# Level products of a gated scan in quarters of the TensorE array, and one place for turning attention's queries

## The chip, the core and the metric

One NeuronCore of a Trainium2 chip runs the whole block as one program. The metric is the device time of one execution in microseconds. A run is one execution; the median of the runs is the time quoted. The profile is one further execution, whose trace is read here.

TensorE (PE) multiplies: a weight load puts one operand into the array, then a matmul streams the other one past it. In the profile the two are PEld and PE. VectorE is DVE, ScalarE is ACT, GpSimd is POOL, and SP issues most of the loads.

## The reference, cut to what matters

A sequence of 256 tokens and a context of 256 tokens pass one block of width 2048: a modulated norm, one wide projection `w_in`, a window attention branch, a gated scan branch in both directions (16 heads of 128), and two output projections that are merged. The change touches the scan and the attention.

```python
def hgrn2_scan(q, k, v, logf, s0):            # forward; the backward one runs on flipped tokens
    def step(S, inp):                         # chunks of 64 tokens
        qc, kc, vc, gc = inp
        G = jnp.cumsum(gc, axis=2)
        o_inter = einsum('bhtk,bhkv->bhtv', qc * jnp.exp(G), S)
        decay = jnp.exp(jnp.where(causal, G_t - G_s, -jnp.inf))
        A = einsum('bhtk,bhsk,bhtsk->bhts', qc, kc, decay)
        o = o_inter + einsum('bhts,bhsv->bhtv', A, vc)
        ...
o = o_f + flip(o_b)                           # hgrn2_bidir
...
q = apply_axial_rope(aq, cos, sin) * HEAD_DIM ** -0.5      # window_attention: 16 heads,
p = softmax(q k^T over 256 tokens in a window + 256 of context, with a sink)   # 4 key heads
att_branch = (p v) * silu(ag)
```

What counts for the change is the matrix A, queries by keys, in both directions at once. Each of its entries carries the decay between its two tokens.

## The kernel before, in words

Every projection takes a weight chunk in `wchunk`: SP loads it, ACT rounds it to a high part `wh`, DVE subtracts to get the low part `wl`, and PE runs three products for each output (`mm3`, lines 82 to 84). All of PE's instructions stand in the order in which the code emits them. The other engines' order comes from the scheduler, which goes by priority.

**The scan.** `pair` handles two heads at a time, so there are 8 pairs. It is a generator: at each `yield` the caller `weave` emits so many projection matmuls of the next pair (the filler), and then the pair goes on. The 256 tokens of two heads make four blocks of 128 by 128 on A's diagonal (index `a`), and four blocks off the diagonal. `AT` holds all eight, keys on the partitions. The diagonal blocks are built in levels: level `b` holds the products of keys and queries in sibling blocks of `b` tokens inside one block of `2b`; level 0 is a token with itself. `grow` multiplies the decay of one more level into queries and keys on DVE; `copies` sets aside on ACT what a level needs.

A level is made by `level` on PE and stored by `keep`. In PSUM the tiles are called `al`. Before the change a level is 8 matmuls: for each `a`, two halves of the array (`tile_position` 0 and 64), 64 keys by 64 queries of fp32. The trace shows an fp32 matmul as two records, so a level is 16 records of PE and 16 of PEld. A pair has two stretches of PE with four levels each: 0, 1, 2, 4 and then 8, 16, 32, 64. `keep` writes the level straight into its place in `AT`: ACT copies levels 0 and 64, one instruction for each half, and DVE writes the others through a mask `mk` (line 570), also one for each half. After the second stretch come four matmuls for the blocks off the diagonal (lines 661 and 662), an ACT copy of them (line 665), 1.5 steps of filler, and then the outputs `ob` (line 677), which read `AT`.

**The attention.** `attend` walks over 32 steps (4 groups of 4 heads, 2 halves of the tokens), and at each yield one piece of `fill` is emitted. A step computes scores `sc`; two steps later its probabilities are turned (`tkp`), and every fourth step multiplies them by the values into `oba`. `group_in(j)` is the filler for group `j`: 8 chunks of the query projection, then 8 of the gate projection. The queries get their rotation on DVE (`rope`), and `turn_q(t)` turns them on PE into the PSUM tile `tkq`, for both halves `t`; ACT and DVE then split that tile into `qTa` (lines 925 and 926). `tkq` and `oba` take turns in the one PSUM buffer with the tag `o`: whichever comes next on PE waits until the one ahead has been read. The table `TURNS` says after which of the 8 gate chunks each half is turned, for each group.

Of the kernel before, what the change touches and what calls it, by code (L numbers as in the profile page):

```python
# [19 lines left out]
EPS = 1e-6  # L20
NEG = -3.0e38
PRIO = 100000
# [8 lines left out]
K_SIN = K_COS + 2 * HD  # L31
K_TRI = K_SIN + 2 * HD
K_END = K_TRI + 2 * P
LEVELS = (1, 2, 4, 8, 16, 32, 64)


@with_exitstack
def block_kernel(ctx: ExitStack, tc: tile.TileContext, x, c, cx, c_ctx, w_ada, b_ada, norm_gain, w_in,
                 b_merge, lb_f, lb_b, hg_gain, w_oh, sink, w_oa, w_out, fin_gain, cst, msk, out):
    nc = tc.nc  # L40
    pe, act, dve, pool = nc.tensor, nc.scalar, nc.vector, nc.gpsimd
# [116 lines left out]

    cs = few.tile([P, K_END], F32, name="cs")
    ident = cs[:, K_ID: K_ID + P]  # L160
    mk = pad.tile([P, 8, P], U8, name="mk")
    mhalf = pad.tile([P, 8], F32, name="mhalf")
    pool.memset(mhalf, -0.5)

# [54 lines left out]
    with pl("st", reuse_waits="tile") as st:  # L219
        cT = st.tile([P, KT, 32], F32, name="cT")  # L220
        mod = st.tile([P, 2, KT, 2], F32, name="mod")
        rows = st.tile([48, P], F32, name="rows")
# [221 lines left out]
        with tc.manual_schedule(engines={mybir.EngineType.PE, mybir.EngineType.SP}):  # L444
# [4 lines left out]
            hi = proj_tok_g(w_in, C_HI, x_st, range(4))  # L449
            bv0 = result(hi)  # L450
            nc.sync.dma_start(cs[:, P:], cst[:, P:])
        mkf = wp.tile([P, 1024], F32, tag="raw", name="mkf", bufs=4)
        nc.sync.dma_start(mkf, msk)
        dve.tensor_copy(mk.rearrange("p a b -> p (a b)"), mkf)

# [18 lines left out]
    def pair(g, p, grp, F, banks_q):  # L474
# [49 lines left out]
        kslot = {1: Kmt[:, 0], 2: Kmt[:, 1], 4: fc[0], 8: Kmt[:, 0], 16: qk[:, 0], 32: F[0][:, :, :T], 64: accT[:, 1]}  # L524
        qslot = {1: fc[1], 2: accT[:, 1], 8: Kmt[:, 1], 16: qk[:, 1], 32: fc[0]}
# [9 lines left out]
                    else:  # L535
                        act.activation(dst.rearrange("p (n two b) -> p n two b", two=2, b=b), src, AF.Copy)  # L536

        def cut(slot, t0):

            return slot[:, t0 // T, t0 % T: t0 % T + 64] if len(slot.shape) == 3 else slot[:, t0: t0 + 64]  # L540

        def level(al, z, b):

            for a in range(4):
                for c in range(2):
                    s0 = a * P + 64 * c
                    t0 = s0 if b < 64 else a * P + 64 * (1 - c)
                    o = al[64 * c: 64 * c + 64, z * 256 + a * 64: z * 256 + a * 64 + 64]  # L550
                    if b == 0:
                        ky, mv = ksum[:, s0: s0 + 64], qT[:, s0: s0 + 64]
                    elif b in qslot:
                        ky, mv = cut(kslot[b], s0), cut(qslot[b], t0)
                    else:
                        ky = cut(kslot[b], s0)
                        o = o.rearrange("p (n two b) -> p n two b", two=2, b=b)
                        mv = mix(1, 1, t0, 64, b)
                    pe.matmul(o, ky, mv, start=True, stop=True, tile_position=(0, 64 * c))  # L559

        def keep(al, z, b):
            for c in range(2):
                hf = slice(64 * c, 64 * c + 64)
                tf = hf if b < 64 else slice(64 * (1 - c), 64 * (1 - c) + 64)
                src = al[hf, z * 256: z * 256 + 256].rearrange("p (a b) -> p a b", a=4)
                if b in (0, 64):
                    act.activation(AT[hf, 0:4, tf], src, AF.Copy)
                else:
                    m = mk[hf, LEVELS.index(b), tf].unsqueeze(1).to_broadcast([64, 4, 64])
                    dve.copy_predicated(AT[hf, 0:4, tf], m, src)  # L570

        tots = {}

# [31 lines left out]
            tots[2 * b] = Tn  # L605

        AT = X2[:, :1024].rearrange("p (a t) -> p a t", a=8)
        TT = X2[:, 1024:]

        def al_bank():  # L610
            return ps.tile([P, 512], F32, tag=alt(), name="al")
# [30 lines left out]
        grow(2)  # L642
        copies(4)
        yield 1.5
        a1, a2 = al_bank(), al_bank()
        for al, z, b in ((a1, 0, 0), (a1, 1, 1), (a2, 0, 2), (a2, 1, 4)):
            level(al, z, b)
        for b in (4, 8, 16, 32):
            grow(b)
            copies(2 * b)  # L650
        grow(64)
        for al, z, b in ((a1, 0, 0), (a1, 1, 1), (a2, 0, 2), (a2, 1, 4)):
            keep(al, z, b)
        yield 3.0
        a3, a4 = al_bank(), al_bank()
        for al, z, b in ((a3, 0, 8), (a3, 1, 16), (a4, 0, 32), (a4, 1, 64)):
            level(al, z, b)
        a5 = ps.tile([P, 512], F32, tag="o", name="al")
        for i in range(2):
            t0, t1 = slice(i * T, i * T + P), slice(i * T + P, (i + 1) * T)  # L660
            pe.matmul(a5[:, 2 * i * P: (2 * i + 1) * P], A[:, 0, t0], A[:, 2, t1], start=True, stop=True)
            pe.matmul(a5[:, (2 * i + 1) * P: (2 * i + 2) * P], A[:, 3, t1], A[:, 1, t0], start=True, stop=True)
        for al, z, b in ((a3, 0, 8), (a3, 1, 16), (a4, 0, 32), (a4, 1, 64)):
            keep(al, z, b)
        act.activation(AT[:, 4:8, :], a5.rearrange("p (a b) -> p a b", a=4), AF.Copy)
        grow(128)
        yield 1.5
# [202 lines left out]
    with tc.manual_schedule(engines={mybir.EngineType.PE}):  # L870
# [25 lines left out]
        for t in range(4):  # L896
            rows = slice(8 + 2 * t, 10 + 2 * t)
# [9 lines left out]
                split(dst[0], dst[1], tk.rearrange("p (j t) -> p j t", j=4))  # L907
                yield

        TURNS = ((1, 3), (1, 4), (0, 3), (2, 4))

        def group_in(j, st):

            bq = yield from proj_tok_g(w_in, C_Q + 512 * j, x_st, range(2))
            def turn_q(t):
                qr = base.tile([P, 4, HD], F32, tag="bb", name="qr", bufs=2)
                rope(qr, bq[t], t)
                yield  # L920
                tk = ps.tile([P, 512], F32, tag="o", name="tkq")
                for i in range(4):
                    pe.transpose(tk[:, i * P: (i + 1) * P], qr[:, i, :], ident)
                qh, ql = [X[:, t].rearrange("p h t -> p (h t)") for X in st["q"]]
                act.activation(qh, tk, AF.Copy, scale=HD ** -0.5)
                dve.scalar_tensor_tensor(ql, tk, HD ** -0.5, qh.bitcast(F32), op0=ALU.mult, op1=ALU.subtract)

            turning = [turn_q(t) for t in range(2)]
            next(turning[0])
            st["q"] = [at.tile([P, 2, 4, P], F32R, tag=tg, name="qTa") for tg in Q_TAGS[j % 2]]  # L930
            st["g"] = gt_tile(j, [P, 4, T], "ga")
            for hf in range(2):
                bg = proj_col_x_g(w_in, C_G + 512 * j + 256 * hf)
                for k0 in range(0, KT, 4):
                    next(bg)
                    yield
                    if (hf, k0) == (0, 0):
                        next(turning[1])
                    for t in range(2):
                        if 4 * hf + k0 // 4 == TURNS[j][t]:  # L940
                            next(turning[t], None)
                for i, b in enumerate(result(bg)):
                    gs = halves_sum(b, "bb", 2)
                    gi = st["g"][:, 2 * hf + i, :]
                    act.activation(gi, gs, AF.Sigmoid)
                    dve.tensor_tensor(gi, gi, gs, op=ALU.mult)
# [139 lines left out]
    for k0 in range(0, KT, 4):  # L1086
        raw, _ = wload(w_out, k0 * P, 4, (D - 256,), 256)
# [10 lines left out]
    for t in range(2):  # L1098
# [7 lines left out]
        for c0, c1, on_act in ((0, 512, True), (512, 1024, False), (1024, 1536, True), (1536, D, False)):  # L1106
# [12 lines left out]
def _constants():  # L1119
    import numpy as np  # L1120

    cst = np.zeros((P, K_END), np.float32)
    cst[:, K_ID: K_ID + P] = np.eye(P, dtype=np.float32)
    tok = np.arange(T)
    row, col = (tok // 64).astype(np.float32), (tok % 64).astype(np.float32)
    inv = (1.0 / (np.float32(10000.0) ** (np.arange(0, 64, 2, dtype=np.float32) / np.float32(64)))).astype(np.float32)
    ar, ac = row[:, None] * inv[None], col[:, None] * inv[None]
    ang = np.concatenate([ar, ar, ac, ac], axis=-1).astype(np.float32)
    sign = np.repeat(np.array([-1, 1, -1, 1], np.float32), 32)
    cos, sin = np.cos(ang), np.sin(ang) * sign  # L1130
    for t in range(2):
        cst[:, K_COS + t * HD: K_COS + (t + 1) * HD] = cos[t * P: (t + 1) * P]
        cst[:, K_SIN + t * HD: K_SIN + (t + 1) * HD] = sin[t * P: (t + 1) * P]
    i, j = np.arange(P)[:, None], np.arange(P)[None, :]
    cst[:, K_TRI: K_TRI + P] = np.where(i >= j, 0.0, NEG)
    cst[:, K_TRI + P: K_TRI + 2 * P] = np.where(j >= i, 0.0, NEG)
    msk = np.zeros((P, 8, P), np.float32)
    for n, b in enumerate(LEVELS):
        msk[:, n] = (i // (2 * b) == j // (2 * b)) & (i // b != j // b)
    return cst, msk.reshape(P, 8 * P)  # L1140


# [27 lines left out]
```

## Time and profile before

| | before |
|---|---|
| median of 3 runs | 1663.74 us |
| lowest, highest | 1663.3, 1664.22 us |
| the profiled execution: its own time | 1663.35 us |
| its span, first to last instruction | 1661.6 us |
| mean granted TensorE clock | 0.995 |
| PE busy | 1631.7 us, 98% |
| DVE busy, ACT busy | 968.2 us, 744.7 us |

The scan's pairs lie between 200 and 910 us of the span, the attention between 1090 and 1460 us. Busy PE is what the matmuls' modelled ends cover: it can be busy and still run faster or slower, so the starts of its matmuls are read below, not only its busy time.

### The profile page before, as it was taken

To read this page: it belongs to the slowest core of one execution; us is meant where nothing else is said; L and a number is where in the kernel's file an instruction comes from. 1 tells how busy PE (TensorE), PEld (TensorE's weight loads), DVE (VectorE), ACT (ScalarE), POOL (GpSimd) and SP (SyncE) were. 2 spreads that over 40 slices of the span, in tenths; PEclk is the share of its full clock that TensorE was granted. 3 is DMA by queue.
4 is the path that set the end of the run, shared out by engine and by line. 5 is a ranking of instruction groups with operands and counts; after the bars stand their busy time and mean duration, and the time that the engine had idled before them with its cause. 6 is when DMAs were issued, how large, how long until landed. Compare 5 with 4: busy or idle time off the path is not lost.

```text
span 1661.6 us, 22807 instructions
## 1 busy us (share of the span) xinstructions
PE 1631.7 (98%) x8889; PEld 1346.9 (81%) x8889; DVE 968.2 (58%) x1503; ACT 744.7 (45%) x1133; POOL 34.8 (2%) x88
## 2 busy tenths in 40 slices
PE   7999999999999999999999999999999999999998
PEld 4558888888888888888888888888878878888887
DVE  4444577546665466745677455325667667555665
ACT  4333444324442344423455443224676767444443
POOL 2000000000000000000000000000000000000000
PEclk9999999999999999999999999999999999999999
DMA  9993444346343553435445556334534445665554
GB/s 354 381 386 108 151 141 140 102 135 191 93 126 116 161 169 102 129 113 176 105 129 171 182 190 194 123 102 145 173 119 149 131 144 159 213 215 190 188 191 140
DMA packets 191436, 275.22 MB, mean 166 GB/s; under 512 B 9808, under 2 KB 112480, under 8 KB 190560
## 3 DMA queue, kind: packets, MB, share of 16 engines
q1 hardware_dynamic: 189344, 269.39, 50.9%
q0 software_dynamic: 1264, 3.25, 1.0%
q8 instruction: 70, 1.15, 0.3%
q10 hardware_dynamic: 720, 1.11, 0.2%
q14 instruction: 38, 0.31, 0.1%
HBM read 271.61 MB, written 2.11 MB: 165 GB/s over the span
## 4 chain that ended last, share of the span: by engine, by line
PE 94%; DMA 3%; ACT 1%; DVE 1%; issue 1%; POOLq 0%; POOL 0%; SPq 0%; ACTq 0%
PE pj L82 23%; PE pj L84 23%; PE pj L83 23%; PE pj L140 7%; PE pj L145 4%; DMA raw<-in_w_ada_dram 3%; PE al L559 2%; PE pa L304 1%; PE pj L394 1%; PE sb L636 1%; PE tkp L978 1%; PE pj L387 1%; PE pj L388 1%; DMA X<-in_x_dram 0%; PE ob L677 0%
## 5 line engine op out<-in xcount | busy, mean ns | idle before, releaser
L76 DVE TENSOR_TENSOR wl<-raw,wh 128x1024 fp32r<-128x1024 f32 x392 | 479.3, 1223 | 432.4 <-ACT wh L75 431.9
L75 ACT ACTIVATE wh<-raw 128x1024 fp32r<-128x1024 f32 x392 | 414.8, 1058 | 590.6 <-PE pj L84 419.5
L83 PE MATMUL pj<-wl,xHL 128*128 128x512 f32 (+1 forms) x1024 | 395.5, 386 | 0.4 <-DVE wl L76 0.4
L84 PE MATMUL pj<-wh,xHL 128*128 128x512 f32 (+1 forms) x1024 | 395.4, 386 | 0.0
L82 PE MATMUL pj<-wh,xHL 128*128 128x512 f32 (+1 forms) x1024 | 391.0, 390 | 0.0
L84 PEld LDWEIGHTS pj<-wh,xHL 128*128 128x128 f32 x1024 | 192.4, 188 | 39.1
L83 PEld LDWEIGHTS pj<-wl,xHL 128*128 128x128 f32 x1024 | 192.5, 188 | 38.2 <-DVE wl L76 0.7
L82 PEld LDWEIGHTS pj<-wh,xHL 128*128 128x128 f32 x1024 | 192.2, 188 | 38.0 <-DVE yt L1034 0.4
L140 PE MATMUL pj<-xHL,wh 128*128 128x512 f32 x512 | 183.3, 400 | 0.0
L82 PE MATMUL pj<-xHL,wh 128*128 128x512 f32 x416 | 164.3, 395 | 0.0
L84 PE MATMUL pj<-xHL,wl 128*128 128x512 f32 x416 | 162.1, 390 | 0.0
L83 PE MATMUL pj<-xHL,wh 128*128 128x512 f32 x416 | 162.0, 390 | 0.0
L145 PE MATMUL pj<-xHL,wl 128*128 128x256 f32 x512 | 140.7, 285 | 0.0
L140 PEld LDWEIGHTS pj<-xHL,wh 128*128 128x128 f32 x512 | 96.4, 191 | 20.4
L145 PEld LDWEIGHTS pj<-xHL,wl 128*128 128x128 f32 x512 | 98.1, 192 | 2.7
L83 PE MATMUL pj<-wl,bH 128*128 128x512 f32 x256 | 99.9, 390 | 0.0
L84 PE MATMUL pj<-wh,bL 128*128 128x512 f32 x256 | 99.7, 389 | 0.0
L84 PEld LDWEIGHTS pj<-xHL,wl 128*128 128x128 f32 x416 | 78.1, 188 | 16.4
L83 PEld LDWEIGHTS pj<-xHL,wh 128*128 128x128 f32 x416 | 78.2, 188 | 15.5
L82 PEld LDWEIGHTS pj<-xHL,wh 128*128 128x128 f32 x416 | 78.2, 188 | 15.6
L82 PE MATMUL pj<-wh,bH 128*128 128x512 f32 x256 | 89.9, 390 | 0.1
L602 DVE TENSOR_TENSOR A<-A,X 128x512 f32<-128x512 f32 x96 | 62.0, 688 | 15.9 <-ACT so L536 6.1
(272 smaller groups left out, 1737.9 us busy)
## 6 DMA issues: line engine op xcount, KB each, us to landing
raw<-in_w_in_dram SPq DMA_DIRECT2D x292, 512.0 KB, 3.6
raw<-in_w_ada_dram SPq DMA_DIRECT2D x128, 256.0 KB, 5.5
raw<-in_w_ada_dram SPq DMA_DIRECT2D x32, 512.0 KB, 3.8
raw<-in_w_o_hgrn_dram SPq DMA_DIRECT2D x32, 512.0 KB, 3.7
raw<-in_w_o_attn_dram SPq DMA_DIRECT2D x32, 512.0 KB, 3.9
raw<-in_w_out_dram SPq DMA_DIRECT2D x32, 512.0 KB, 4.4
raw<-in_w_in_dram SPq DMA_DIRECT2D x24, 256.0 KB, 5.4
X<-in_x_dram SPq DMA_DIRECT2D x2, 1024.0 KB, 6.4
```

What stands on the lines that cost most here:

```text
L75: act.activation(h[:, :n], raw[:, :n], AF.Copy)
L76: dve.tensor_tensor(lo[:, :n], raw[:, :n], h[:, :n].bitcast(F32), op=ALU.subtract)
L82: pe.matmul(o, s[0], m[0], start=first, stop=False)
L83: pe.matmul(o, s[0], m[1], start=False, stop=False)
L84: pe.matmul(o, s[1], m[0], start=False, stop=last)
L140: pe.matmul(banks[i].rearrange("p (a t) -> p a t", a=2), h[:, j, cs_], xHL[:, :, kt, :T], start=kt == 0, stop=kt == KT - 1)
L145: pe.matmul(banks[i][:, :T], lo[:, j, cs_], xH[:, kt, :T], start=False, stop=False)
L304: pe.matmul(pa[32 * g: 32 * g + 32, : 2 * w], cT[:, k0 + g, :], rv_[:, :, g % nk, :], start=k0 == 0, stop=k0 == KT - 4, tile_position=(0, ...
L387: pe.matmul(o, hw, xH[:, kt, :], start=kt == 0, stop=False)
L388: pe.matmul(o, lo[:, kt - k, cs_], xH[:, kt, :], start=False, stop=False)
L559: pe.matmul(o, ky, mv, start=True, stop=True, tile_position=(0, 64 * c))
L602: dve.tensor_tensor(av, av, f.unsqueeze(3).to_broadcast([P, 2, n2, b]), op=ALU.mult)
```

## The change

Two things are changed.

**The levels.** Levels 0 to 32 become products of 32 keys by 32 queries, 16 matmuls in place of 8, in four quarters of the array (`tile_position` 0, 32, 64, 96). Level 32 pairs each 32 keys with the 32 queries of the sibling quarter. Level 64 becomes 16 matmuls of 32 keys by 64 queries. The results of levels 0 to 32 no longer go to their place in `AT`: all of them go to a compact tile `near`, 128 partitions by 4 by 64, which lies where `AT[:, 4:6]` will be. One instruction stores a level: ACT for levels 0 and 32, DVE with the mask for 1, 2, 4, 8, 16. The mask shrinks from 8 by 128 to 5 by 32 columns. A new function `spread` then copies `near` into `AT` on ACT with 8 instructions, one for each quarter and each of its two parts, ahead of the copy of the off-diagonal blocks. Level 64 still goes straight into `AT`. The four levels of the first stretch share one PSUM bank, and levels 8, 16, 32 another.

**The queries.** `TURNS` is gone: in each group the halves are turned after the gate chunks 1 and 3. Before it was (1, 3), (1, 4), (0, 3), (2, 4) for the groups 0 to 3. The two instructions that split `tkq` now stand at a raised priority.

```diff
-LEVELS = (1, 2, 4, 8, 16, 32, 64)
+LEVELS = (1, 2, 4, 8, 16)
...
-    mk = pad.tile([P, 8, P], U8, name="mk")
+    mk = pad.tile([P, len(LEVELS), 32], U8, name="mk")
...
-        def level(al, z, b):
+        def level(al, c0, b):
+            n = 64 if b == 64 else 32
             for a in range(4):
-                for c in range(2):
-                    s0 = a * P + 64 * c
-                    t0 = s0 if b < 64 else a * P + 64 * (1 - c)
-                    o = al[64 * c: 64 * c + 64, z * 256 + a * 64: z * 256 + a * 64 + 64]
+                for g in range(4):
+                    s0 = a * P + 32 * g
+                    t0 = a * P + (32 * (g ^ 1) if b == 32 else 64 * (1 - g // 2) if b == 64 else 32 * g)
+                    o = al[32 * g: 32 * g + 32, c0 + a * n: c0 + a * n + n]
...
-                    pe.matmul(o, ky, mv, start=True, stop=True, tile_position=(0, 64 * c))
+                    pe.matmul(o, ky, mv, start=True, stop=True, tile_position=(0, 32 * g))
...
+        def keep(al, c0, b):
+            if b == 64:
+                ...                                   # two ACT copies into AT, as before
+            src = al[:, c0: c0 + P].rearrange("p (a b) -> p a b", a=4)
+            if b in (0, 32):
+                act.activation(near[:, :, b: b + 32], src, AF.Copy)
+            else:
+                m = mk[:, LEVELS.index(b), :].unsqueeze(1).to_broadcast([P, 4, 32])
+                dve.copy_predicated(near[:, :, 0:32], m, src)
+        def spread():
+            for g in range(4):
+                rows = slice(32 * g, 32 * g + 32)
+                for z in range(2):
+                    c0 = 32 * (g ^ z)
+                    act.activation(AT[rows, 0:4, c0: c0 + 32], near[rows, :, 32 * z: 32 * z + 32], AF.Copy)
...
+        near = X2[:, 512:768].rearrange("p (a b) -> p a b", a=4)
...
-        TURNS = ((1, 3), (1, 4), (0, 3), (2, 4))
...
-                act.activation(qh, tk, AF.Copy, scale=HD ** -0.5)
-                dve.scalar_tensor_tensor(ql, tk, HD ** -0.5, ...)
+                with tc.high_priority(2 * PRIO):
+                    act.activation(qh, tk, AF.Copy, scale=HD ** -0.5)
+                    dve.scalar_tensor_tensor(ql, tk, HD ** -0.5, ...)
...
-                    for t in range(2):
-                        if 4 * hf + k0 // 4 == TURNS[j][t]:
-                            next(turning[t], None)
+                    if hf == 0 and k0 in (4, 12):
+                        next(turning[k0 // 8], None)
```

How the instructions stand, in three places. First PE in pair 0, second stretch of levels, before (`pj` is the filler's projection, `al` the levels):

```order
L84 MATMUL pj<-xHL,wl 128x512
L559 MATMUL al<-Kmt 64x64 x8
L559 MATMUL al<-qk 64x64 x8
L559 MATMUL al<-ff 64x64 x8
L559 MATMUL al<-so,acc 64x64 x8
L661 MATMUL al<-A 128x128
```

The same place after the change:

```order
L85 MATMUL pj<-xHL,wl 128x512
L562 MATMUL al<-Kmt 32x32 x16
L562 MATMUL al<-qk 32x32 x16
L562 MATMUL al<-ff 32x32 x16
L562 MATMUL al<-so,acc 32x64 x16
L677 MATMUL al<-A 128x128
```

Nothing else of PE's order moves in the scan: twice as many matmuls stand in each level's place, and the filler around them is the same.

Second, ACT in pair 1 behind the second stretch, before (`wh` is a weight chunk's high part, `X` is the buffer that holds `AT`, `sg` belongs to the next pair):

```order
L75 ACTIVATE wh<-raw 128x1024 x2
L665 ACTIVATE X_2250<-al 128x512
L567 ACTIVATE X_2250<-al 64x4x64 x2
L209 ACTIVATE sg<-pj 128x512
L75 ACTIVATE wh<-raw 128x1024
```

and after:

```order
L76 ACTIVATE wh<-raw 128x1024 x2
L569 ACTIVATE X_2315<-al 64x4x64 x2
L574 ACTIVATE X_2315<-al 128x4x32
L584 ACTIVATE X_2315<-X_2315 32x4x32 x8
L682 ACTIVATE X_2315<-al 128x512
L211 ACTIVATE sg<-pj 128x512
L76 ACTIVATE wh<-raw 128x1024
```

Nine instructions have come in between the level copies and `sg`, and the copy of the off-diagonal blocks now stands last.

Third, PE in attention group 1, where its second half of queries is turned, before:

```order
L83 MATMUL oba<-pT,xHL 128x512
L84 MATMUL oba<-pT,xHL 128x512
L978 MATMUL tkp<-cs,pr 128x128 x4
L923 MATMUL tkq<-cs,qr 128x128 x4
L145 MATMUL pj<-xHL,wl 128x256
```

and after:

```order
L83 MATMUL sc<-xHL,qTa 128x512
L84 MATMUL sc<-xHL,qTa 128x512
L85 MATMUL sc<-xHL,qTa 128x512
L936 MATMUL tkq<-cs,qr 128x128 x4
L141 MATMUL pj<-xHL,wh 128x512
```

`tkq` stood right behind `oba` and one turn of probabilities; it now stands behind the scores, 13 projection matmuls ahead of that same `oba`. Group 3 moves in the same way. In group 2 the second half stood there already, and only the first half moves.

Last, ACT in group 2 behind its second `tkq`, before (`ga` is the output gate, `pr` the probabilities):

```order
L945 ACT_TABLE_LOAD
L945 ACTIVATE ga<-hsum 128x256
L968 ACTIVATE pr<-pr,mx 128x512
L925 ACTIVATE qTa<-tkq 128x512
L154 ACTIVATE hsum<-pj 128x256
```

and after:

```order
L958 ACT_TABLE_LOAD
L958 ACTIVATE ga<-hsum 128x256
L939 ACTIVATE qTa<-tkq 128x512
L155 ACTIVATE hsum<-pj 128x256
L977 ACT_TABLE_LOAD
```

`qTa` has moved ahead of the scaling of `pr`. Groups 1 and 3 now have this order too.

More of the change, by code (lines that the diff above doesn't have):

```diff
@@ L160, in block_kernel @@
     ident = cs[:, K_ID: K_ID + P]
-    mk = pad.tile([P, 8, P], U8, name="mk")
+    mk = pad.tile([P, len(LEVELS), 32], U8, name="mk")
+    pad.tile([P, 216], F32, name="space0")
     mhalf = pad.tile([P, 8], F32, name="mhalf")
@@ L451, in block_kernel @@
             nc.sync.dma_start(cs[:, P:], cst[:, P:])
-        mkf = wp.tile([P, 1024], F32, tag="raw", name="mkf", bufs=4)
+        mkf = wp.tile([P, 1024], F32, tag="raw", name="mkf", bufs=4)[:, : 32 * len(LEVELS)]
         nc.sync.dma_start(mkf, msk)
@@ L536, in copies, with cut @@
                         act.activation(dst.rearrange("p (n two b) -> p n two b", two=2, b=b), src, AF.Copy)
-        def cut(slot, t0):
-            return slot[:, t0 // T, t0 % T: t0 % T + 64] if len(slot.shape) == 3 else slot[:, t0: t0 + 64]
-        def level(al, z, b):
+        def cut(slot, t0, n):
+            return slot[:, t0 // T, t0 % T: t0 % T + n] if len(slot.shape) == 3 else slot[:, t0: t0 + n]
+        def level(al, c0, b):
+            n = 64 if b == 64 else 32
             for a in range(4):
-                for c in range(2):
-                    s0 = a * P + 64 * c
-                    t0 = s0 if b < 64 else a * P + 64 * (1 - c)
-                    o = al[64 * c: 64 * c + 64, z * 256 + a * 64: z * 256 + a * 64 + 64]
[L551 to L559, printed above, removed]
@@ L561, in keep @@
-        def keep(al, z, b):
-            for c in range(2):
[L563 to L570, printed above, removed]
+                for g in range(4):
+                    s0 = a * P + 32 * g
+                    t0 = a * P + (32 * (g ^ 1) if b == 32 else 64 * (1 - g // 2) if b == 64 else 32 * g)
+                    o = al[32 * g: 32 * g + 32, c0 + a * n: c0 + a * n + n]
+                    if b == 0:
+                        ky, mv = ksum[:, s0: s0 + 32], qT[:, t0: t0 + 32]
+                    elif b in qslot:
+                        ky, mv = cut(kslot[b], s0, 32), cut(qslot[b], t0, n)
+                    else:
+                        ky = cut(kslot[b], s0, 32)
+                        o = o.rearrange("p (n two b) -> p n two b", two=2, b=b)
+                        mv = mix(1, 1, t0, n, b)
+                    pe.matmul(o, ky, mv, start=True, stop=True, tile_position=(0, 32 * g))
@@ new lines, in keep @@
+        def keep(al, c0, b):
+            if b == 64:
+                for c in range(2):
+                    hf = slice(64 * c, 64 * c + 64)
+                    act.activation(AT[hf, 0:4, 64 * (1 - c): 64 * (2 - c)],
+                                   al[hf, c0: c0 + 256].rearrange("p (a b) -> p a b", a=4), AF.Copy)
+                return
+            src = al[:, c0: c0 + P].rearrange("p (a b) -> p a b", a=4)
+            if b in (0, 32):
+                act.activation(near[:, :, b: b + 32], src, AF.Copy)
+            else:
+                m = mk[:, LEVELS.index(b), :].unsqueeze(1).to_broadcast([P, 4, 32])
+                dve.copy_predicated(near[:, :, 0:32], m, src)
@@ L644, in pair @@
         yield 1.5
-        a1, a2 = al_bank(), al_bank()
-        for al, z, b in ((a1, 0, 0), (a1, 1, 1), (a2, 0, 2), (a2, 1, 4)):
-            level(al, z, b)
+        a1 = al_bank()
+        for z, b in enumerate((0, 1, 2, 4)):
+            level(a1, z * P, b)
         for b in (4, 8, 16, 32):
@@ L651, in pair @@
         grow(64)
-        for al, z, b in ((a1, 0, 0), (a1, 1, 1), (a2, 0, 2), (a2, 1, 4)):
-            keep(al, z, b)
+        for z, b in enumerate((0, 1, 2, 4)):
+            keep(a1, z * P, b)
         yield 3.0
         a3, a4 = al_bank(), al_bank()
-        for al, z, b in ((a3, 0, 8), (a3, 1, 16), (a4, 0, 32), (a4, 1, 64)):
-            level(al, z, b)
+        for al, c0, b in ((a3, 0, 8), (a3, P, 16), (a3, 2 * P, 32), (a4, 0, 64)):
+            level(al, c0, b)
         a5 = ps.tile([P, 512], F32, tag="o", name="al")
@@ L662, in pair @@
             pe.matmul(a5[:, (2 * i + 1) * P: (2 * i + 2) * P], A[:, 3, t1], A[:, 1, t0], start=True, stop=True)
-        for al, z, b in ((a3, 0, 8), (a3, 1, 16), (a4, 0, 32), (a4, 1, 64)):
-            keep(al, z, b)
+        for al, c0, b in ((a3, 0, 8), (a3, P, 16), (a3, 2 * P, 32), (a4, 0, 64)):
+            keep(al, c0, b)
+        spread()
         act.activation(AT[:, 4:8, :], a5.rearrange("p (a b) -> p a b", a=4), AF.Copy)
@@ L924, in turn_q @@
                 qh, ql = [X[:, t].rearrange("p h t -> p (h t)") for X in st["q"]]
-                act.activation(qh, tk, AF.Copy, scale=HD ** -0.5)
-                dve.scalar_tensor_tensor(ql, tk, HD ** -0.5, qh.bitcast(F32), op0=ALU.mult, op1=ALU.subtract)
+                with tc.high_priority(2 * PRIO):
+                    act.activation(qh, tk, AF.Copy, scale=HD ** -0.5)
+                    dve.scalar_tensor_tensor(ql, tk, HD ** -0.5, qh.bitcast(F32), op0=ALU.mult, op1=ALU.subtract)
             turning = [turn_q(t) for t in range(2)]
@@ L1136, in _constants @@
     cst[:, K_TRI + P: K_TRI + 2 * P] = np.where(j >= i, 0.0, NEG)
[L1137 to L1140, printed above, removed]
+    s, t = i % 32, j[:, :32]
+    msk = np.stack([(s // (2 * b) == t // (2 * b)) & (s // b != t // b) for b in LEVELS], 1).astype(np.float32)
+    return cst, msk.reshape(P, 32 * len(LEVELS))
 def kernel(**inputs):
```

## The prediction

> **What bounds the kernel now.** First the page, for who is busy and what the chain that ended last consists of; then the busy time by stage; then what PE waited for.
>
> ```profile
> span 1661.6 us, 22807 instructions
> PE 1631.7 (98%) x8889; PEld 1346.9 (81%) x8889; DVE 968.2 (58%) x1503; ACT 744.7 (45%) x1133; POOL 34.8 (2%) x88
> ...
> PE 94%; DMA 3%; ACT 1%; DVE 1%; issue 1%; POOLq 0%; POOL 0%; SPq 0%; ACTq 0%
> ```
>
> ```profile
> 200.00:910.00 710.00, 709.44 (x4357) 599.61 (x4357) 447.46 (x700) 303.56 (x501) 19.00 (x48) 1.00 0.45 135
> 1090.00:1460.00 370.00, 360.47 (x1775) 301.80 (x1774) 230.82 (x395) 216.53 (x338) 3.29 (x6) 0.99 0.49 152
> ```
>
> ```profile
> PE tkq L923 <- DVE br L988: 8.3, 2, 4.1
> ...
> PE oba L82 <- DVE qTa L926: 0.8, 1, 0.8
> PE ob L677 <- ACT X L567: 0.6, 1, 0.6
> ```
>
> PE carries 94% of the chain. In the scan (first stage row; the columns are length, then PE, PEld, DVE, ACT and POOL busy) it idles 0.6 of 710 us, so there a microsecond less of PE is a microsecond less of time, as long as DVE (63%) and ACT (43%) keep up. In the attention (second row) it idles 9.5 of 370 us, and two waits of `tkq` make up 8.3 of that. The change aims at both places.
>
> **The levels on PE.** The first stretch of levels in pair 1, between two projections:
>
> ```profile
> 283.11 0.39 PE L84 MATMUL pj<-xHL,wl 128*128 128x512 f32 x1
> 283.43 0.69 PE L559 MATMUL al<-qk 128*64 128x64 f32 x16
> 283.94 0.64 PE L559 MATMUL al<-F,Kmt 128*64 128x64 f32 x16
> 284.41 0.64 PE L559 MATMUL al<-acc,Kmt 128*64 128x64 f32 x16
> 284.88 0.64 PE L559 MATMUL al<-A,ff 128*64 128x64 f32 x16
> 285.44 0.50 PE L82 MATMUL pj<-xHL,wh 128*128 128x512 f32 x1
> ```
>
> From start to start a level takes 0.47 us: 16 records, 29 ns each. The kernel already has a product in 32-wide quarters, the modulation (line 304), and it shows whether quarters work side by side:
>
> ```profile
> 26.07 1.13 PE L290 MATMUL prs<-dgx,onesx 128*128 128x512 f32 x2
> ```
>
> ```profile
> 36.23 0.64 PE L304 MATMUL pa<-raw,cT 128*32 128x512 f32 x4
> ```
>
> ```profile
> 36.23 1.92 PE L304 MATMUL pa<-raw,cT 128*32 128x512 f32 x16
> ```
>
> ```profile
> 36.23 0.16 PEld L304 LDWEIGHTS pa<-raw,cT 128*32 128x32 f32 x8 [0.36 <-DMA raw<-in_w_ada_dram]
> ```
>
> ```profile
> L304 PEld LDWEIGHTS pa<-raw,cT x16: 106/109/110, 36.2 to 37.1; 128*32 128x32 f32 x16
> ```
>
> On the full array two fp32 records of 512 columns take 1.13 us, one behind the other. In quarters four of them take 0.64 us and sixteen 1.92 us: all four quarters stream at once. Groups of four follow each other every (1.92 - 0.64) / 3 = 0.43 us, or 0.83 ns per column. Eight weight loads of 0.11 us each lie within 0.16 us, so they too run at once, and eight were started, with four matmuls between them, in 0.16 - 0.11 = 0.05 us.
>
> By the same reading the halves before the change run two at a time: 8 groups in 0.47 us, 58 ns each, of which 64 x 0.83 = 53 ns is streaming and 5 ns is fixed. A group of four quarters with 32 columns then takes 27 + 5 = 32 ns, and a level of 32 records has 8 such groups: 0.25 us. The price of a 32-column record is not in the trace, so it gets bounds: 0.235 us a level if all of it goes by length, and 0.47 us, no gain, if a group of short matmuls takes what a group of long ones does. I take 0.25, since the 512- and 64-column rows lie on one line with a small fixed part. Seven levels (0 to 32) in 8 pairs save 0.22 us each: **-12.3 us** (bounds -13.2 and 0). Level 64 keeps 64 columns and 8 groups: 0. Going into and out of the narrow array (283.11 to 283.43, and the 0.56 us from the last level to the next projection) happens as often as before.
>
> On the issue side 32 records in 0.25 us are 7.8 ns each. The eight loads above were started 6 to 7 ns apart, with matmuls in between. That is just enough, and it is the thinnest spot of this sum; a rival below starts there.
>
> **The store of the levels.** DVE and ACT are hidden behind filler here, if the output `ob` does not come to wait. Pair 1, behind its second stretch of levels:
>
> ```profile
> 304.26 2.34 DVE L570 COPY_PREDICATED X<-mk,al 64x256 f32<-64x256 uint8 x5
> ...
> 307.28 0.45 DVE L570 COPY_PREDICATED X<-mk,al 64x256 f32<-64x256 uint8 x1
> ```
>
> ```profile
> 305.26 0.60 ACT L665 ACTIVATE X<-al 128x512 f32<-128x512 f32 x1 [2.28 <-PE al L662]
> 307.76 0.77 ACT L567 ACTIVATE X<-al 64x256 f32<-64x256 f32 x2 [1.91 <-DVE X L570]
> ```
>
> ```profile
> 310.47 0.38 PE L677 MATMUL ob<-v,X 128*128 128x128 f32 x2
> ```
>
> ```profile
> L536 ACT ACTIVATE Kmt<-A 128x512 f32<-128x512 f32 x32 | 21.8, 706 | 26.2 <-DVE A L602 20.0 <-DVE A L589 4.2 <-DVE A L510 2.1
> ...
> L533 ACT ACTIVATE F<-A 128x256 f32<-128x256 f32 x50 | 19.1, 443 | 13.4 <-DVE A L602 13.4
> ```
>
> Before, `AT` is ready at 308.53 and `ob` starts at 310.47: 1.9 us to spare. After, DVE has two masked copies of 128 columns in place of six of 256 (each no more than the 0.45 us of a wide one), from 304.26 to 305.1 at the latest. ACT has copied level 64 while DVE worked; then come level 32, eight copies of `spread` and the off-diagonal copy. The two ACT rows give 1.03 ns per column, so a 128-column copy costs 0.31 us (they may be less, back to back): nine make 2.8 us, and with 0.6 for the last copy `AT` is ready at 308.5. `ob` itself comes 3 x 0.22 = 0.66 us earlier, at 309.8. That leaves 1.3 us: **0**. What stands behind these copies in ACT's queue is the next pair's `sg`, at 308.56 before, and the weight roundings behind it; they are not later. In all DVE loses 3.8 us a pair or so and ACT gains about 2. The smaller mask is one load and one cast, off the chain. In pair 2 the wait of 0.6 us in the list above ended with ACT behind DVE's last masked copy; with four copies fewer it may go. I count it only in the low end.
>
> **The queries.** One of the two stalls, and the clock after each:
>
> ```profile
> 1224.49 0.60 PE L978 MATMUL tkp<-cs,pr 128*128 128x128 f32 x4
> 1229.22 0.94 PE L923 MATMUL tkq<-cs,qr 128*128 128x128 f32 x4 [4.13 <-DVE br L988]
> ```
>
> ```profile
> 1229.20:1233.00 3.80, 3.78 (x14) 3.37 (x15) 1.38 (x2) 1.14 (x2) 0.00 (x0) 0.55 0.00 0
> ...
> 1355.60:1359.40 3.80, 3.80 (x15) 3.37 (x16) 1.39 (x2) 1.09 (x2) 0.00 (x0) 0.55 0.02 4
> ```
>
> `tkq` wants the buffer that `oba` has just filled, and DVE's `br` reads it only 4 us later. After each stall PE runs 3.8 us at a granted clock of 0.55 (the column behind POOL), which costs 3.8 x 0.45 = 1.7 us more. In the new order `tkq` stands ahead of that `oba` in groups 1 and 3, so this wait is gone: -8.3 - 3.4 = -11.7 us. What is late next is `oba`, which must now wait until ACT and DVE have read `tkq`. Group 2 shows that order already:
>
> ```profile
> 1287.56 0.40 PE L140 MATMUL pj<-xHL,wh 128*128 128x512 f32 x1
> 1288.72 0.50 PE L82 MATMUL oba<-pT,xHL 128*128 128x512 f32 x1 [0.76 <-DVE qTa L926]
> ```
>
> ```profile
> 1285.13 1.28 ACT L945 ACT_TABLE_LOAD   x1
> 1286.42 0.42 ACT L945 ACTIVATE ga<-hsum 128x256 f32<-128x256 f32 x1
> 1286.75 0.71 ACT L968 ACTIVATE pr<-pr,mx 128x512 f32<-128x512 f32 x1
> 1287.36 0.58 ACT L925 ACTIVATE qTa<-tkq 128x512 fp32r<-128x512 f32 x1
> ```
>
> The projection ahead starts at 1287.56 and `oba` 1.16 us later, where projections follow each other in 0.23: 0.9 us lost. ACT had scaled `pr` (0.61 us from start to start) before it read `tkq`. In the changed order that scaling stands behind, in all three groups, so I take 0.9 - 0.6 = 0.3 us for each: group 2 gains 0.6, groups 1 and 3 lose 0.3 each, together 0. The bounds are no wait at all (-0.9) and the full 0.9 in three groups (+1.8). The weight roundings that now stand behind `qTa` and the scores' exponential on ACT serve a chunk two ahead, so PE does not meet them at once. Queries: **-11.7 us** (-12.6 to -9.9).
>
> **The sum.** The profiled execution took 1663.35 us, 0.4 under the median of the runs. 1663.35 - 12.3 - 11.7 = 1639.4, and on the median's scale 1639.8: I say **1640 us**. With the bounds of the costs alone: 1663.7 - 13.2 - 12.6 - 0.6 = 1637 to 1663.7 - 0 - 9.9 = 1654.
>
> **The rivals.** A change under 0.2% (3.3 us) is about what a measurement of this kernel cannot tell from none.
>
> *Short matmuls cost what long ones do.* If a record of 32 columns holds its quarter for the 58 ns of one with 64, the levels gain nothing and the time is 1663.7 - 11.7 = 1652. For it: nothing in the trace is shorter than 64 columns in a narrow array. Against it: the fixed part is 5 of 58 ns. The Trainium skill, TensorEngine Tiling (Array Packing), Instruction Overhead, speaks for a weaker form: some 60 cycles for each matmul, the same at 1 column as at 60, and it warns against tiling a dimension that is small already. At the 2.4 GHz of the Trainium skill, TensorE: Matmul & The Clock Gate, What's actually happening, two passes of 60 cycles make a group 50 ns, and the time would be an estimated 1648.3 us. No row here shows the floor either way. Chance 16%.
>
> *The array takes records one after the other.* If each record of a level starts no sooner than 29 ns behind the last (what the rows above show, read as an issue rate and not as two halves at work), a level of 32 records takes 0.94 us. Then 8 levels in 8 pairs cost 64 x 0.47 = 30 us more, and the kernel ends at 1663.7 + 30 - 11.7 = 1682: slower. It turns from gain to loss where a record costs (0.47 + 11.7 / 64) / 32 = 20 ns. Against it stand the eight loads started in 0.05 us; for it, that these are a short burst behind a wait, and a stretch has 128 records. Chance 9%.
>
> *Quarters pair up, but not four at a time* (short work, two streams): 16 groups of 32 ns are 0.51 us a level, 2 us lost in all, 1654. The modulation's rows speak against it. Chance 4%.
>
> *The stall moves on.* ACT is near full at the ends of attention groups (three table loads of 1.28 us), and PE arrives there some 6 us earlier than before. If `oba` or a weight chunk then waits 2 us in each of the three groups, 6 of the 11.7 us are lost: 1646. Or `spread` ends more than 1.3 us later than I have it, and `ob` waits in 8 pairs, 1 us each: 1648. Against both: DVE is 62% busy there and the loads had run so far ahead that no byte moved after the stall (0 GB/s in the row above). Chance 12%.
>
> My forecast, 1637 to 1643, has the remaining 59%. From 1637 to 1655 all but the slower rival and a few per cent are covered. Faster by over 0.2%: 59 + 16 + 4 + 12, less 3 for mixtures of them: 88%. Slower: 9%. Within: 3%.
>
> **What would show it.** Right: a level from start to start in 0.25 us, PE with 1024 records more but less busy time; no wait of `tkq`, the clock at 1.00 throughout the attention, and `oba` waiting well under 1 us. Wrong: a level at 0.4 us or more; `ob` waiting for ACT in most pairs; a clock under 1 in the attention, or a new wait over 2 us at the groups' ends.

## The result, and the profile after

The changed kernel takes 1649.49 us (median of five runs, 1646.69 to 1650.36), the kernel before 1663.58 us beside it: a ratio of 0.991, 95% interval 0.990 to 0.993. That is 14.1 us less. It lies outside the 1637 to 1643 of the forecast proper, 9.5 us above its 1640, and inside the 1637 to 1655 that took in most of the rivals. The profiled execution took 1650.36 us, 13.0 less than the one of before. First the page, then the two stages:

```profile
span 1648.6 us, 24835 instructions
...
PE 1621.8 (98%) x9913; PEld 1336.3 (81%) x9913; DVE 934.4 (57%) x1447; ACT 763.4 (46%) x1199; POOL 31.9 (2%) x88
```

```profile
200.00:910.00 710.00, 703.77 (x5391) 592.81 (x5390) 415.86 (x647) 320.97 (x566) 14.89 (x48) 0.99 0.45 136
1090.00:1460.00 370.00, 369.03 (x1828) 308.49 (x1827) 236.39 (x400) 224.92 (x347) 3.29 (x6) 1.00 0.51 160
```

In the attention PE now idles 1.0 of 370 us (9.5 before). In the scan it is the other way round: 6.2 of 710 us idle, where it was 0.6. The list of PE's waits names both:

```profile
PE al L562 <- issue: 6.1, 3, 2.8
...
PE oba L83 <- DVE qTa L940: 0.5, 3, 0.2
```

`tkq` is gone from it, and something new stands there: PE stops three times inside a level product, for 6.1 us, and no semaphore releases it ("issue" is time in which the engine waited for nothing that the profile shows).

The levels themselves, same place as before (pair 1, first stretch):

```profile
282.04 0.46 PE L562 MATMUL al<-qk 128*32 128x32 f32 x32
282.31 0.46 PE L562 MATMUL al<-F,Kmt 128*32 128x32 f32 x30
...
282.88 0.45 PE L562 MATMUL al<-A,ff 128*32 128x32 f32 x30
283.26 0.50 PE L83 MATMUL pj<-xHL,wh 128*128 128x512 f32 x1
```

```profile
300.71 0.65 PE L562 MATMUL al<-so,acc 128*32 128x64 f32 x32
301.29 0.49 PE L677 MATMUL al<-A 128*128 128x128 f32 x2
```

A level takes 0.27 us from start to start, 8 groups of four of 34 ns; it was 0.47. Level 64 keeps its price (0.58 against 0.56). The first stretch is 1.22 us long, the second (299.83 to 301.29) 1.46; each was 2.01 before. A pair saves 1.34 us, eight pairs 10.7.

The stores behind the second stretch of pair 1:

```profile
301.48 0.77 ACT L569 ACTIVATE X<-al 64x256 f32<-64x256 f32 x2 [0.66 <-PE al L562]
301.99 0.63 DVE L577 COPY_PREDICATED X<-mk,al 128x128 f32<-128x128 uint8 x2
302.83 2.53 ACT L584 ACTIVATE X<-X 32x128 f32<-32x128 f32 x8
305.44 0.60 ACT L682 ACTIVATE X<-al 128x512 f32<-128x512 f32 x1
...
307.75 0.38 PE L694 MATMUL ob<-v,X 128*128 128x128 f32 x2
```

`spread` takes 2.53 us for its eight copies, `AT` is ready at 306.04 and `ob` starts 1.7 us later. The line of `ob` has left the list of waits too (0.6 us in pair 2 before).

Now the stall. It stands in pair 6, in the last level of the first stretch:

```profile
809.79 0.22 PE L562 MATMUL al<-A,F 128*32 128x32 f32 x2 [0.58 <-issue]
812.84 0.62 PE L562 MATMUL al<-A,F 128*32 128x32 f32 x6 [2.83 <-issue]
816.14 0.58 PE L562 MATMUL al<-A,F 128*32 128x32 f32 x12 [2.67 <-issue]
```

```profile
816.60:821.90 5.30, 5.30 (x19) 4.14 (x13) 3.40 (x7) 2.37 (x5) 0.00 (x0) 0.50 0.64 182
```

The stretch starts at 807.77 and the next projection at 816.65: 8.88 us for what takes 1.22 elsewhere, 7.7 lost. Then PE runs at a granted clock of 0.50 for 5.3 us, its projections 0.43 us apart and not 0.23; that is some 2.4 us more. Together 10 us. The bill of the two profiled executions closes with it: -10.7 for the levels, -11.9 for the queries (measured alone below), -0.6 for `ob`, +10.0, in all -13.2, and 13.0 were measured. All other level stretches, in this pair and in the others, run without a gap over 0.16 us.

### The profile page after: what moved, and what is told of

It is laid out like the page before. It is cut to its first block, busy times and chain, and to the rows that moved or that the text cites. A ratio compares the mean times of both kernels' runs of the same rounds, so it can differ in the third digit from the quotient of the medians.

```text
span 1648.6 us, 24835 instructions
## 1 busy us (share of the span) xinstructions
PE 1621.8 (98%) x9913; PEld 1336.3 (81%) x9913; DVE 934.4 (57%) x1447; ACT 763.4 (46%) x1199; POOL 31.9 (2%) x88
## 4 chain that ended last, share of the span: by engine, by line
PE 94%; DMA 4%; DVE 1%; issue 1%; ACT 0%; SPq 0%; POOLq 0%; POOL 0%; ACTq 0%
PE pj L83 23%; PE pj L85 23%; PE pj L84 23%; PE pj L141 7%; PE pj L146 3%; DMA raw<-in_w_ada_dram 3%; PE al L562 1%; PE pa L306 1%; PE sb L652 1%; PE tkp L991 1%; DMA X<-in_ctx_dram 1%; PE pj L396 1%; PE pj L389 0%; PE oba L83 0%; PE ob L694 0%
```

## The experiments

Ratios are to the kernel before, run beside each.

**Each part alone.** The levels with the old turns, and the turns with the old levels:

```diff
 e1: the changed kernel, but
+        TURNS = ((1, 3), (1, 4), (0, 3), (2, 4))
 ...                          (and tkq split at its old priority)
-                    if hf == 0 and k0 in (4, 12):
-                        next(turning[k0 // 8], None)
+                    for t in range(2):
+                        if 4 * hf + k0 // 4 == TURNS[j][t]: ...
 e2: the kernel before, with the opposite of these lines
```

> The levels alone, attention as before. Theory (an issue stall in pair 6 that only the longer level stretch meets): 7 levels in 8 pairs save 0.20 us each, 11 us, and the stall with its cold clock gives about 9 back: 1661 to 1663 us, with a gap of 5 us or more inside the first level stretch of pair 6. Rival (the missing 9 us belong to the attention or to both changes together): 1652 us, no gap over 1 us in pair 6.

> The queries alone, levels as before. Theory (the query step is as predicted, and the loss lies in the levels): 1652 us, oba waits under 0.5 us in each group, no cold clock in the attention. Rival (the new order of the turns gives part of it back elsewhere): 1656 us or more.

Levels alone: 1660.49 us, ratio 0.9978 (0.9969 to 0.9987), a gain of 3.3 us. Queries alone: 1651.89, ratio 0.9926 (0.9913 to 0.9938), a gain of 11.9. PE's waits of the first, then of the second:

```profile
PE tkq L937 <- DVE br L1002: 8.3, 2, 4.1
...
PE al L562 <- issue: 5.4, 2, 4.9
```

```profile
PE ob L677 <- ACT X L567: 0.7, 1, 0.7
...
PE oba L82 <- DVE qTa L926: 0.5, 3, 0.2
```

So the loss lies in the levels alone, and the queries give what they were said to.

**Two first attempts.** GpSimd issues two things just ahead of that stretch. One is `gate_rows`, a store of 128 by 16 numbers, turned on the way, so 2048 elements of 4 bytes each (line 778); it is read only near the end, at 1407 us. The other are two bias rows, 256 KB each, broadcast to all partitions (line 465).

```profile
804.58 1.26 POOL L778 DMA_DIRECT2D gate_rows<-gcol  x1 [95.93 <-DVE gcol L206]
806.41 0.30 POOL L464 COPY bb<-F 128x1 f32<-128x1 f32 x2 [0.57 <-DVE F L212]
806.93 1.13 POOL L465 DMA_DIRECT2D bb<-in_b_merge_dram  x2 [0.22 <-POOL bb L464]
```

A second suspect was the supply of instructions. The page shows a DMA queue of that kind (packets, MB, share of the engines' time):

```profile
q8 instruction: 78, 1.28, 0.3%
```

That is 16 KB a packet. PE has 9913 matmuls, as many loads and some 110 others, so a packet for each 256 of them, and in the trace one packet does come whenever about 256 have started. A stretch now issues exactly 256 instructions, records and loads, in 1.22 us. I call the places where a packet is due boundaries; the one in pair 6 falls on about the stretch's 200th instruction, and PE stops after the 215th.

```diff
 e3: the changed kernel, with the store's line moved behind the loop over the pairs
-        nc.gpsimd.dma_start(gate_rows.rearrange("k p -> p k"), gcol)
 ...
+        nc.gpsimd.dma_start(gate_rows.rearrange("k p -> p k"), gcol)
 e4: the kernel before, behind rest(16)
+            for q in range(40):
+                pe.transpose(few_idle[:32, ...], ident[:32, :32], ident[:32, :32])
```

> The changed kernel, with one DMA of GpSimd (gate_rows, 2048 elements of 4 bytes, needed only near the end) issued after the last pair and not just ahead of pair 6's levels. Theory A (PE's instruction supply stalls where a packet boundary falls while this scattered store holds up the DMA rings): no stall in pair 6, 1640 to 1642 us. Theory B (the two bias rows behind it on the same queue do it): stall stays, 1649 us. Theory C (quarters run out of instructions by themselves): stall stays, 1649 us.

> The kernel before, with 40 small transposes more (32 by 32, 80 instructions, about 1 us) early in the program, so that PE's packet boundary near 831 us falls into pair 6's first level stretch, near 818 us. Theory A (boundary while the scattered store is under way): the kernel before gets the stall too, 5 us or more without a semaphore inside or just behind that stretch, 1670 us or more. Rival (the stall belongs to the quarter products): 1664 to 1665 us, no such gap.

The first says nothing: the scheduler put the store back to 804.61 us, since nothing but its source held it.

```profile
804.61 1.26 POOL L843 DMA_DIRECT2D gate_rows<-gcol  x1 [95.93 <-DVE gcol L206]
```

It is one more measurement of the changed kernel: 1648.59 us, stall as before. The second took 1663.77 us, ratio 0.9999 (0.999 to 1.0008). The boundary lay on about the 110th of the stretch's 128 instructions, and the packet due there near 818 us came at 830.3; PE had no gap in that time. A boundary is not enough, then, and neither is a packet 12 us late. Nor is the store, for the kernel before issues it just as far ahead of the same stretch, which starts at 816.41:

```profile
813.23 1.26 POOL L761 DMA_DIRECT2D gate_rows<-gcol  x1 [95.28 <-DVE gcol L204]
```

**Bias rows, store or boundary.** Here the bias rows were moved by what they wait for, and the store was tied to the last pair's result, so that the scheduler could not pull it back.

```diff
 e5: bias rows behind group 3's gate (774 us)
-                    biases[0, m] = bias_row(0, m, res[0][0][:, 0, 0:1])
+                    biases[0, m] = bias_row(0, m, grps[3][2][:, 0, 0:1])
 e6: store behind the last pair (gc2 a new tile)
+        pool.tensor_copy(gc2[:, 0:1], bH[:, 15, 0:1].bitcast(F32))
+        pool.tensor_copy(gc2, gcol)
+        nc.gpsimd.dma_start(gate_rows.rearrange("k p -> p k"), gc2)
 e7: bias rows ahead of pair 4
-            if n == 7:
+            if n == 5:
 e8: 64 small transposes behind rest(16), as in e4, but in the changed kernel
```

> The changed kernel with the two bias rows of GpSimd's queue (256 KB each, broadcast to 128 partitions) loaded some 34 us earlier, behind the last gate of group 3 near 774 us, where no level stands. The small scattered store (gate_rows) stays at 804.6 us. Theory B (the bias rows' transfer is what stops PE in pair 6): no gap over 1 us in the levels, no cold clock behind them, 1640 to 1642 us. Theory A (the scattered store does it): stall stays, 1649 us. Theory C (quarters run out of instructions at that place by themselves): 1649 us.

> The changed kernel with the scattered store tied to the last pair's result (two small GpSimd copies more), so that it really leaves its place, to about 935 us; the bias rows stay at 807 us. Theory A: no stall in pair 6, 1640 to 1642 us. Theory B: the stall stays, some 6 us, 1647 to 1650 us.

> The changed kernel with the bias rows loaded two pairs earlier, just ahead of pair 4's first level stretch (610 us), aligned to it as they were to pair 6's. Theory B: the stall leaves pair 6 and shows in pair 4's first stretch, 5 to 6 us without a semaphore and half a clock behind it, 1647 to 1650 us. Theory C: stall stays in pair 6.

> The changed kernel with 64 small transposes more (128 instructions, about 1 us) early in the program, so that PE's instruction-packet boundary falls into pair 6's first stretch 128 instructions earlier, in its second level and not its fourth. If the stall sits at the boundary: it starts in the second level, near instruction 75 to 90 of the 256. If it comes a fixed time (1.7 us) behind the start of the bias transfer: still in the fourth level, near instruction 213. In both cases about the time of the changed kernel plus 1 us.

e5: 1649.4 us, ratio 0.992 (0.9907 to 0.9934). The store alone is left, and the stall stays:

```profile
806.49 1.19 POOL L778 DMA_DIRECT2D gate_rows<-gcol  x1 [31.43 <-DVE gcol L206]
```

```profile
812.63 0.19 PE L562 MATMUL al<-A,F 128*32 128x32 f32 x1 [1.51 <-issue]
815.64 0.48 PE L562 MATMUL al<-A,F 128*32 128x32 f32 x17 [2.82 <-issue]
```

e7: 1649.59 us in a single run; no gap in pair 4, and 6.4 us of stall in pair 6. The bias rows are out. e8: 1651.17 us in a single run. The boundary now lay on about the stretch's 75th instruction; the stall still began behind the 219th, in the last level (its first row):

```profile
814.73 0.50 PE L565 MATMUL al<-A,F 128*32 128x32 f32 x7 [3.70 <-issue]
```

So my reading by boundaries was wrong. In all these kernels PE stops 4.1 to 4.4 us behind the issue of the store, which is also 210 to 220 instructions into the stretch.

e6 has no gap in pair 6, which is what theory A said, but it took 1657.58 us in its single run. The loss stands at the other end of the program: PE waited ten times for a load of the modulation's weights, and its first level stretches came some 11 us late.

```profile
PE pa L306 <- DMA raw<-in_w_ada_dram: 4.5, 10, 1.0
```

Its late store also costs a wait of 2.6 us behind the last pair, which the next run shows more closely. Whether the new tile, which moves others, or something outside disturbed the start, this run cannot say, so the next one does without the tile.

**The store late, and the levels later.**

```diff
 e9: as e6, but
-        gc2 = pad.tile([P, 16], F32, name="gc2")
+        gc2 = space0[:, :16]
 ...
 e10: the changed kernel, ahead of the first level stretch
-        yield 1.5
+        yield 2.0
```

> The changed kernel with the scattered store (gate_rows) tied to the last pair's result, as in the run before, but with its source in the unused tile space0, so that no tile moves; nothing else differs. Theory A (the scattered store starves PE's instruction supply, and only a level stretch of 256 instructions in 1.25 us is fast enough to feel it): no gap over 1 us in pair 6, clock 1.00 there, 1640 to 1642 us. Rival (the run before lost its stall only because its start was disturbed): stall at 809 to 816 us, 1649 us.

> The changed kernel with one weight chunk more of filler (2.0 for 1.5 steps, 12 projections, 2.7 us) ahead of each first level stretch; the scattered store stays where the gates end, so that pair 6's stretch starts 5.9 us behind the store's issue and not 3.2. If the supply fails a fixed time (4.1 to 4.4 us) behind the issue: the stretch runs dry at once, within its first 60 instructions, or already in the projections ahead. If PE lives on a stock of some 230 instructions from the store on: it runs dry near instruction 190 to 213 as before. If 2.7 us are enough for the store to drain: no stall, 1641 us. Otherwise 1647 to 1651 us.

e9: 1646.89 us, ratio 0.9891 (0.9875 to 0.9908). The stretch of pair 6 takes its 1.22 us again, its last level without idle time inside:

```profile
810.92 0.45 PE L562 MATMUL al<-A,F 128*32 128x32 f32 x30
```

The start is quieter too (0.7 us of waits for those loads). But the time is not 1640, for the store, now issued behind the last pair, hits something else there. DMA issues between 930 and 960 us, of the late store and then of the changed kernel (the last number is the time from issue to landing):

```profile
raw<-in_w_o_hgrn_dram SPq DMA_DIRECT2D x1, 512.0 KB, 15.2
gate_rows<-space POOLq DMA_DIRECT2D x1, 8.0 KB, 11.8
```

```profile
raw<-in_w_o_hgrn_dram SPq DMA_DIRECT2D x4, 512.0 KB, 3.6
```

```profile
PE pj L83 <- ACT wh L76: 2.5, 1, 2.5
```

A weight chunk of 512 KB takes 15.2 us beside the store, 3.6 without it, and PE waits 2.5 us for it, and then runs slowly: the granted clock is 0.76 on average from 948.8 to 956.0 us. The store does harm at another place, this time with a name in the profile.

e10 did not do what I wanted: the fillers of earlier pairs moved along with the levels, and the store still stands 3.2 us ahead of pair 6's stretch. 1647.82 us in a single run, 4.5 us of stall. So in every run that stalls the store is issued 3.2 us ahead of the stretch.

**What a shorter record costs.** Built on e9; it leaves out half of the products of the levels 0 to 8:

```diff
-            n = 64 if b == 64 else 32
+            n = 64 if b == 64 else 16 if b < 16 else 32
 ...
```

> The late-store kernel with levels 0, 1, 2, 4 and 8 cut to the first 16 of the 32 queries (the other half of these products is left out): what a still shorter record costs. By length (0.7 to 0.83 ns a column and a fixed 7 to 12): 18 to 21 ns a group of four, a level of 8 groups in 0.15 to 0.17 us. If records start no closer than 6.5 ns: 26 ns a group, 0.21 us. If a group has a floor at what 32 columns take: 32 to 34 ns, 0.27 us.

```profile
282.48 0.45 PE L562 MATMUL al<-qk 128*32 128x16 f32 x32
282.75 0.43 PE L562 MATMUL al<-F,Kmt 128*32 128x16 f32 x30
...
283.31 0.43 PE L562 MATMUL al<-A,ff 128*32 128x16 f32 x30
283.68 0.51 PE L83 MATMUL pj<-xHL,wh 128*128 128x512 f32 x1
```

0.27 us from level to level, the stretch 1.20 us and not 1.22: half the columns cost the same. The third outcome is right, a floor. Whether it is a floor of a group or of the issue this run does not tell: with each record comes a load, so PE issues eight instructions for each group. (Its 1644.14 us in a single run has e9's gap at 944 us too.)

**The store in rows.** The last kernel stores the same numbers as 16 rows. Turning them takes time, so the store now stands ahead of pair 6's second stretch, while the bias rows stay just ahead of its first:

```diff
 e12, in gates()
-        nc.gpsimd.dma_start(gate_rows.rearrange("k p -> p k"), gcol)
+        yield
+        gT = ps.tile([P, 512], F32, tag="tp", name="tqr")
+        pe.transpose(gT[:KT, :P], gcol, ident)
+        act.activation(space0[:KT, :P], gT[:KT, :P], AF.Copy)
+        nc.gpsimd.dma_start(gate_rows, space0[:KT, :P])
```

> The changed kernel with the gates turned once more on PE (one transpose, one ACT copy of 16 by 128) and stored as 16 rows of 512 bytes, not 2048 elements of 4; the store is issued some 4 us ahead of pair 6's second level stretch, about as far as the scattered one stood ahead of the first. Theory A (it is the scattering that holds up other transfers and starves PE): no stall in either stretch of pair 6, clock 1.00, 1640 to 1642 us. If any store of GpSimd's queue near a level stretch does it: the stall shows in the second stretch, 1647 to 1650 us.

1640.51 us (1640.23 to 1641.83), ratio 0.986 (0.984 to 0.987): 23.3 us faster than before, 9 faster than the change, and the fastest kernel of this study. The last level of pair 6's first stretch, then the store and the second stretch behind it:

```profile
810.11 0.45 PE L562 MATMUL al<-A,F 128*32 128x32 f32 x30
```

```profile
823.54 0.52 POOL L782 DMA_DIRECT2D gate_rows<-space  x1 [13.93 <-ACT space L781]
```

```profile
827.16 0.46 PE L562 MATMUL al<-Kmt 128*32 128x32 f32 x32
827.44 0.46 PE L562 MATMUL al<-qk 128*32 128x32 f32 x30
```

DMA issues between 800 and 830 us, here, and then of the changed kernel with the bias rows moved (e5) and of the levels alone (e1):

```profile
bb<-in_b_merge_dram POOLq DMA_DIRECT2D x2, 256.0 KB, 4.0
gate_rows<-space POOLq DMA_DIRECT2D x1, 8.0 KB, 1.6
```

```profile
gate_rows<-gcol POOLq DMA_DIRECT2D x1, 8.0 KB, 13.1
```

```profile
bb<-in_b_merge_dram POOLq DMA_DIRECT2D x2, 256.0 KB, 13.8
gate_rows<-gcol POOLq DMA_DIRECT2D x1, 8.0 KB, 11.9
```

The same 8 KB land after 1.6 us as 16 rows of 512 bytes, and after 11.9 to 13.1 us as 2048 elements; the bias rows take 4.0 us behind the one and 13.8 behind the other. Issued 3.6 us ahead of a level stretch, the store in rows costs PE nothing; but it has landed 2.0 us before that stretch begins, so no run has the store in rows under way beside one. The bias rows, issued on the same queue 0.8 us ahead of the first stretch, land 3.1 and 3.8 us after it has begun, and PE does not stop there.

## Why the prediction was right, and where it was short

**Levels, -12.3 us: right in kind, measured 10.7.** The mis-sized term is the level: 0.27 us and not 0.25, a group of four 34 ns and not 32, and leaving the narrow array takes a little more. The working behind it was wrong, though it came out near. I drew a line through 512 and 64 columns and read 27 ns of streaming and 5 fixed at 32. With 16 columns that line gives 18 ns, and the run shows the same 0.27 us a level. What sets a short group is a floor of 33 to 34 ns, four records 8 ns apart on average, and 32 columns happen to lie just at it: that the estimate came within 2 ns is luck. The rival "short matmuls cost what long ones do" is refuted at its price (34 ns, not the 58 of 64 columns), and so are the serial array and the pairs: records start 8 ns apart on average, near the 6 to 7 of the eight loads of the modulation.

The Trainium skill stood behind a weaker form of that rival. The Trainium skill, TensorEngine Tiling (Array Packing), Instruction Overhead, says that a matmul has about 60 cycles of overhead and costs the same at 1 column as at 60. The run with 16 columns bears out that there is a floor; by the estimate I made from its figure a group would take 50 ns, and the rows show 34. That the 1648.3 us of this estimate lie near the measured time is chance.

**The stores, 0: right.** `AT` was ready 1.7 us ahead of `ob` in pair 1 (I had 1.3), and the 0.6 us of pair 2 went, as the low end allowed.

**The queries, -11.7 us: right.** 11.9 alone. Both waits of `tkq` are gone, with the cold clock behind them, and `oba` loses 0.3 us in each of three groups, as said. Its first row, PE ahead and `oba` 0.56 us behind it where 0.23 is usual:

```profile
1220.55 0.69 DVE L940 SCALAR_TENSOR_TENSOR qTa<-tkq,qTa 128x512 fp32r<-128x512 f32 x1
...
1220.74 0.40 PE L141 MATMUL pj<-xHL,wh 128*128 128x512 f32 x1
...
1221.30 0.50 PE L83 MATMUL oba<-pT,xHL 128*128 128x512 f32 x1 [0.16 <-DVE qTa L940]
```

**What the sum left out: 9 to 10 us.** Levels and queries together make 22.6 us, and 1663.7 - 22.6 = 1641.1; the kernel with the store in rows takes 1640.51. The point forecast was thus the time of the change without the stall. That the wide range held is luck: the rivals opened it, and none of them is what happened. The measured 1649.49 lies near the 1648 of a late `spread`, but no wait of `ob` is in the trace. The step that failed is the one on the issue side: "That is just enough, and it is the thinnest spot of this sum." I asked there whether the array takes records 7.8 ns apart, which it does in all sixteen stretches. I did not ask what else 256 instructions in 1.22 us might depend on, nor what runs beside each stretch, and so the sum has nothing for it. GpSimd's store stood in the trace of before, 3.2 us ahead of pair 6's stretch, and I never looked at that queue. "The stall moves on" was the nearest rival, but it looked for the new wait on ACT and DVE, at the groups' ends and at `ob`; the new wait over 2 us that I had named as a sign of error came in the scan, on no semaphore.

What the runs show: with the scattered store 3.2 us ahead, a stretch in quarters stalls (the change and e1, e3, e5, e7, e8, e10), and halves do not (before, and e4). Without it there, nothing stalls, with the bias rows where they were. With the same bytes stored as rows, nothing stalls. What they don't show is the link between. In the six of these runs whose trace has the landing of the store (e1, e3, e5, e7, e8, e10), the stall begins and ends while the store is under way. Other queues are held up in that time: a weight load that SP issues at 810.04 us in the changed kernel lands after 12.6 us, its neighbours after 3.4 to 3.5, and the instruction packet due at 809 us starts at 822.3. But that packet is not what PE waited for, since PE was at work again at 816.14, 6 us before it, and in e4 a packet came as late with no gap. That PE lacks instructions is thus no more than a reading of "issue", and in the simple form, one late packet, the traces and e8 speak against it. What PE waited for stays open. Whether the stall begins a fixed time behind the store or after a stock of some 210 instructions stays open too, since both kept their distance in every run, and no run put the scattered store ahead of another pair's stretch.

## What to carry to other kernels

When a change makes an engine issue the same work in more and shorter instructions, look at what else moves beside each of those bursts, DMAs of idle queues included, for what cost the longer instructions nothing may stop the shorter ones. A stall on "issue" inside one tile's work, at one place of many alike, points to such a neighbour: change the neighbour, not the stalled work. Moved, the store did harm at its new place; in another form it did none. And what is moved must be moved by a true dependence, since the scheduler here put back what only the program's text had moved.

## What was not expected of the hardware

- A DMA of 8 KB in 4-byte elements takes 11.8 to 13.2 us to land, and other transfers with it: 13.8 us for bias rows that take 4.0, 15.2 for a weight chunk that takes 3.6. As 512-byte rows it lands after 1.6 us. The Trainium skill, DMA: Bandwidth & Descriptors, Why small descriptors are slow (HBM only), gives a fixed cost for each packet. The trace counts 48 packets for the store in elements (e5) and 32 for the rows (e12), so a cost of that kind does not make 13.1 us of 1.6. That other queues' transfers are held up for as long, and that PE stops meanwhile, it does not say there, and these runs show it.
- In quarters of the array an fp32 group of four takes 34 ns with 32 columns and the same with 16, against 58 for a pair of halves with 64: cutting the columns from 64 to 32 paid, from 32 to 16 it paid nothing.
- After 7 us of broken work PE ran 5.3 us at a granted clock of 0.50, so a stall of this length costs a third more than it shows.
